# One decoder block on one core: how many expert rows go ahead of the second search, how densely they come in it, and on which engine

## The chip, the core and the metric

The kernel runs on one core of a Trainium2 chip, from a single launch. The time is the device time of that core in microseconds, from three runs. Beside them there is one execution under the hardware profiler. The engines are named as the profile names them: PE is TensorE, DVE is VectorE, ACT is ScalarE, POOL is GpSimd, SP is the engine that issues most transfers.

## What is computed

One decoder block on 512 tokens of width 1024: three token mixers side by side (forgetting attention, sliding-window attention, attention on a memory), merged by gates, and then product-key experts. The last part is what the change touches. For each token and each of 8 heads, 16 of 16384 experts are chosen by two searches over 128 half keys and a search over their sums; each expert is one row of `u` and one row of `v`.

```
s1 = einsum('bshd,hkd->bshk', q[..., 0, :], keys1);  v1, i1 = top_k(s1, 16)
s2 = einsum('bshd,hkd->bshk', q[..., 1, :], keys2);  v2, i2 = top_k(s2, 16)
cand = v1[..., :, None] + v2[..., None, :];          sv, si = top_k(cand, 16)
experts = i1[si // 16] * 128 + i2[si % 16];          gates = softmax(sv)
...
a = einsum('cd,ced->ce', h, u[experts])
out = einsum('ce,ced->cd', gelu(a) * gates, v[experts])
```

So each token has 128 experts. All is in float32.

## The kernel before

The tokens are four blocks of 128. Block 0 goes through the mixers by itself, then blocks 1 to 3 together. Its experts are therefore known early, and while the mixers of the other three run, block 0 is searched and its expert rows are worked off beside them.

**Two ways of doing the experts.** Blocks 0 and 1 gather rows: one indirect transfer of GpSimd's queue (L908) brings one row of `u` or `v` for each of 128 tokens, 512 KB. There are 512 such jobs, in the order block 0 `u` (0 to 127), block 0 `v` (128 to 255), block 1 `u` (256 to 383), block 1 `v` (384 to 511). Blocks 2 and 3 are dense: all 16384 rows of `u` (`dense_u`, L1078, 128 tiles) and of `v` (`dense_v`) are multiplied, and a gate matrix that is zero where an expert was not chosen picks the right ones.

**One row, the function `step`.** It first issues the gathers that may be ahead (four rows ahead of the one being worked off; five slots hold rows), then works off one row. For a row of `u` VectorE does a product with a sum (L929). For a row of `v` VectorE does a multiply-add: into `x1[0]`, which the order and the profile call `mg` and which lies in SBUF, as long as the mixers hold the PSUM banks (L936); after that into `two`, a PSUM tile (the first row writes it, L939, the others add, L942). A row called with `apart` is GpSimd's instead: for `v`, ScalarE scales the row (L932) and GpSimd adds it to `x1[0]` (L933). `two` is added to `x1[0]` after row 255 (L948).

**Stages, by the profile's times.**

- *End of the mixers, 562 to 622 us.* The generator `beside` works off rows up to `EARLY_ROWS`, whenever a weight load calls `pump`. With 184, rows 0 to 183 go here: 128 of `u`, 56 of `v`.
- *Second search, from 622 to about 741 us*, for blocks 1 to 3. For each head and half PE multiplies a weight tile of 512 KB, split into a high and a low part (ScalarE casts `whi`, L123; GpSimd subtracts `wlo`, L136), ScalarE copies the queries `qp` (L770), PE multiplies the keys (L774), ScalarE copies the scores `s` (L777). VectorE finds the best 16 of each (L731 to L735), GpSimd builds the 64 sums `cand` (L742), and VectorE finds the best 16 of those. Four tiles of `dense_u` lie in between.
- *Choosing, 741 to 825 us.* VectorE turns places into expert numbers (L828 to L872) for the three blocks, and 37 rows go among it; PE does `dense_u`.
- *Spreading, 825 to 985 us.* 64 times, VectorE builds one-hot matrices (`o`, L1144), ScalarE scales them (L1147), PE multiplies them (L1159), VectorE (L1162) and ScalarE (L1165) take the result; 60 rows and 23 tiles of `dense_u` go among it. There every fourth row is apart.
- *Final products, 985 us to the end.* 128 steps of `dense_v`, each with its share of what is left of `dense_u` and of the rows: the rows left are spread evenly over 124 steps.

**How often a row comes in the second search.** The search is a generator that names the cost of each piece of VectorE work in units: 1.6 for one block's best 16 of one half, 1.2 for one of the 64 sums. A head has 6 x 1.6 + 3 x 1.2 = 13.2 units, and the eight heads have 105.6. `spent` adds them up; `credit` does as well, and whenever it reaches `PER_ROW`, a row follows and `PER_ROW` is taken off. Each weight load calls `pump`, which finds nothing to do here and sets the credit to zero: that happens at the start of heads 0 to 5, whose turn loads the weights of the head after the next.

**What sets the order.** Up to the end of the search a scheduler places instructions by a simulated timeline; rows in the search have a low priority (`tc.high_priority(-LATER)`), so they fill gaps and may come later than where they were written. From there on POOL, DVE and PE run in the order in which the code is written.

Of the kernel before, what the change touches and what calls it, by code (L numbers as in the profile page):

```python
# [51 lines left out]
UNREAD = 36  # L52
LATER = 400
PACE = {"search": 20.0, "choose": 8.0, "rows": 3.5}
EARLY_ROWS, PER_ROW, APART, NO_APART = 184, 3.7, 4, 94.0
OWN_ROWS = 9


# [1 line left out]
def tile_block(ctx: ExitStack, tc: tile.TileContext, t: dict, out: bass.AP):  # L60
# [160 lines left out]
    def factors(sums, nb):  # L221

        ss = small_f(BIG, "rss", 2)[:, :nb]
        V.reduce_sum(ss, sums[:, :nb], axis=AX.X)
        return rsqrt_mean(ss, nb, D)

    def diagonals(r, nb):
        dg = small.tile([128, BIG, 128], F32, tag="dg", name="dg", bufs=1)
        for b in range(nb):
            A.activation(dg[:, b], ident, AF.Copy, scale=r[:, b:b + 1])  # L230
        return dg
# [646 lines left out]
    known, issued, done, ahead, flying, rpool = [2 * NJ], [0], [0], [AHEAD], {}, []  # L878
# [168 lines left out]
    def fetch_u_to(k):  # L1047
        while u_next[0] <= min(k, NK - 1):
            fetch_u(u_next[0])
            u_next[0] += 1  # L1050
# [36 lines left out]
    with tc.tile_pool(name="qb", bufs=2) as qq:  # L1087
        turn([x1[b] for b in GROUPS[1]], g2, *h2T)
        spent, dg, credit[0] = 0.0, None, 0.0
        for cost in search(qq, h2T, f, BIG):  # L1090
            spent += cost
            if dg is None and spent > 12.0:
                V.tensor_copy(rstd[:, 1:NB], factors(sums, BIG))
                dg = diagonals(rstd[:, 2:NB], ND)
                turn([x1[b] for b in DENSE], g2, h2f, None, dg)
            while u_next[0] < PRE_U and spent > 6.0 * u_next[0]:
                fetch_u_to(u_next[0])
            credit[0] += cost
            while credit[0] >= PER_ROW and NJ <= done[0] < known[0]:
                credit[0] -= PER_ROW  # L1100
                with tc.high_priority(-LATER):
                    step(apart=done[0] % APART == 0 and spent < NO_APART)
            if k_u < FIRST_U and spent > 104.0 / FIRST_U * (k_u + 1):
                list(dense_u(k_u))
                k_u += 1
# [317 lines left out]
```

## Time and profile before

| | |
|---|---|
| runs (us) | 1549.64, 1550.77, 1543.61; median 1549.64 |
| the profiled execution (us) | 1548.8 |
| its span, first to last instruction (us) | 1547.0 |
| mean granted clock of TensorE | 0.99 |
| data moved | 533.48 MB, mean 345 GB/s |
| rows of `v` on VectorE in PSUM (L942) | 197 |
| rows of `v` on GpSimd (L933) | 8 |

The profile gives, for each engine, its busy time in any stretch of the span; what ended each idle time of an engine (its waits); and a timeline of single instructions. A group of instructions is written as line, engine, operation, output and inputs, then how often it ran and how long. A busy TensorE is not TensorE at its peak, since its matmuls overlap and their ends are modelled.

### The profile page before, as it was taken

To read this page: it belongs to the slowest core of one execution; us is meant where nothing else is said; L and a number is where in the kernel's file an instruction comes from. 1 tells how busy PE (TensorE), PEld (TensorE's weight loads), DVE (VectorE), ACT (ScalarE), POOL (GpSimd) and SP (SyncE) were. 2 spreads that over 40 slices of the span, in tenths; PEclk is the share of its full clock that TensorE was granted. 3 is DMA by queue.
4 is the path that set the end of the run, shared out by engine and by line. 5 is a ranking of instruction groups with operands and counts; after the bars stand their busy time and mean duration, and the time that the engine had idled before them with its cause. 6 is when DMAs were issued, how large, how long until landed. Compare 5 with 4: busy or idle time off the path is not lost.

```text
span 1547.0 us, 27092 instructions
## 1 busy us (share of the span) xinstructions
PE 1498.3 (97%) x9411; PEld 1360.5 (88%) x9411; DVE 1419.4 (92%) x2673; ACT 812.4 (53%) x1806; POOL 778.1 (50%) x642
## 2 busy tenths in 40 slices
PE   8999999999999989999999999999999999999998
PEld 7999899997897989999888887788888888888887
DVE  6689488989999999999999999899999999999998
ACT  7778346646345533352225899545444544544543
POOL 1101016767667456877445666545554544555451
PEclk9999999999998999999999999999999999999999
DMA  8688657998999898986998999999999999999995
GB/s 325 207 289 300 246 174 280 338 362 302 360 367 325 293 356 317 352 310 232 327 365 329 393 395 384 373 397 398 401 410 403 408 410 404 411 410 410 410 410 209
DMA packets 180125, 533.48 MB, mean 345 GB/s; under 512 B 17660, under 2 KB 48148, under 8 KB 179988
## 3 DMA queue, kind: packets, MB, share of 16 engines
q0 software_dynamic: 73728, 268.47, 45.9%
q1 hardware_dynamic: 96180, 227.54, 40.1%
q10 hardware_dynamic: 10080, 35.75, 5.8%
q8 instruction: 74, 1.21, 0.3%
q14 instruction: 63, 0.52, 0.1%
HBM read 516.99 MB, written 14.69 MB: 344 GB/s over the span
## 4 chain that ended last, share of the span: by engine, by line
PE 52%; issue 14%; DMA 11%; POOL 9%; DVE 9%; ACT 4%; POOLq 0%; DVEq 0%; SPq 0%; ACTq 0%
PE mm L153 9%; PE mm L152 9%; PE mm L154 9%; POOL row L908 9%; PE mm L1078 5%; DMA row<-in_peer_v_dram,eidx 4%; DMA row<-in_peer_u_dram,eidx 3%; PE sc L1078 3%; DVE wlo L138 2%; DMA gd<-st 2%; PE mm L766 2%; DVE o L1144 2%; DVE scr L929 1%; PE tp L384 1%; PE sc L506 1%
## 5 line engine op out<-in xcount | busy, mean ns | idle before, releaser
L908 POOL DMA_INDIRECT row<-in_peer_v_dram,eidx x256 | 322.2, 1258 | 298.3 <-DVE two L942 175.5
L908 POOL DMA_INDIRECT row<-in_peer_u_dram,eidx x256 | 315.4, 1232 | 219.8 <-DVE scr L929 115.8
L138 DVE TENSOR_TENSOR wlo<-raw,whi 128x1024 fp32r<-128x1024 f32 (+1 forms) x228 | 277.2, 1220 | 21.7 <-ACT whi L123 17.5
L942 DVE SCALAR_TENSOR_TENSOR two<-row,acts,two 128x1024 f32<-128x1024 f32 x197 | 252.6, 1282 | 5.3 <-DMA row<-in_peer_v_dram,eidx 3.1
L123 ACT CAST whi<-raw 128x1024 fp32r<-128x1024 f32 x146 | 152.2, 1050 | 119.2 <-PE mm L153 75.4
L929 DVE SCALAR_TENSOR_TENSOR scr<-row,own 128x1024 bf16<-128x1024 f32 x128 | 156.2, 1220 | 7.1 <-DMA row<-in_peer_u_dram,eidx 6.4
L929 DVE SCALAR_TENSOR_TENSOR scr<-row,two 128x1024 bf16<-128x1024 f32 x115 | 139.5, 1213 | 3.8 <-DMA row<-in_peer_u_dram,eidx 2.9
L210 POOL TENSOR_TENSOR rsy<-rsv,mhalf 128x4 f32<-128x4 f32 (+5 forms) x25 | 37.8, 1515 | 177.2 <-DVE rsv L209 176.3
L1212 ACT CAST ah<-ga 128x256 fp32r<-128x256 f32 x116 | 47.1, 407 | 150.2 <-PE tp L153 125.0
L152 PE MATMUL mm<-hhi,whi 128*128 128x384 f32 x320 | 110.8, 346 | 1.8 <-ACT hhi L244 1.4
L153 PE MATMUL mm<-hlo,whi 128*128 128x384 f32 x320 | 110.7, 346 | 0.0
L154 PE MATMUL mm<-hhi,wlo 128*128 128x384 f32 x320 | 109.9, 343 | 0.0
L152 PE MATMUL mm<-whi,hhi 128*128 128x256 f32 (+1 forms) x360 | 103.6, 290 | 2.7 <-ACT hhi L681 1.9
L1214 ACT CAST whi<-raw 128x1024 fp32r<-128x1024 f32 x96 | 100.3, 1047 | 9.5 <-DMA raw<-in_peer_v_dram 4.6
L153 PE MATMUL mm<-wlo,hhi 128*128 128x256 f32 (+1 forms) x360 | 102.7, 286 | 1.3 <-DVE wlo L138 1.3
L153 PE MATMUL sc<-wlo,ah 128*128 128x512 f32 x256 | 101.2, 395 | 2.5 <-DVE wlo L138 2.5
L152 PE MATMUL sc<-whi,ah 128*128 128x512 f32 x256 | 100.8, 394 | 1.3 <-ACT whi L1214 1.2
L154 PE MATMUL mm<-whi,hlo 128*128 128x256 f32 (+1 forms) x360 | 102.0, 285 | 0.0
L154 PE MATMUL sc<-whi,al 128*128 128x512 f32 x256 | 101.2, 395 | 0.0
L153 PE MATMUL tp<-wlo,ah 128*128 128x512 f32 x256 | 101.1, 395 | 0.0
L152 PE MATMUL tp<-whi,ah 128*128 128x512 f32 x256 | 101.0, 395 | 0.0
L154 PE MATMUL tp<-whi,al 128*128 128x512 f32 x256 | 100.6, 393 | 0.0
(332 smaller groups left out, 4478.2 us busy)
## 6 DMA issues: line engine op xcount, KB each, us to landing
raw<-in_peer_v_dram SPq DMA_DIRECT2D x96, 512.0 KB
hhi<-in_uT_dram ACTq DMA_DIRECT2D x68, 512.0 KB
raw<-in_w_tr_dram SPq DMA_DIRECT2D x48, 512.0 KB
raw<-in_w_nat_dram SPq DMA_DIRECT2D x40, 512.0 KB
last<-in_peer_v_dram SPq DMA_DIRECT2D x32, 512.0 KB
hhi<-in_uT_dram SPq DMA_DIRECT2D x26, 512.0 KB
raw<-in_w_o_dram SPq DMA_DIRECT2D x24, 512.0 KB
gd<-st SPq DMA_DIRECT2D x24, 512.0 KB
```

The costliest lines, as they stand in the source:

```text
L123: ins = (cast or A.copy)(hi[:, :n * w], raw[:, :n * w])
L138: V.tensor_sub(lo, raw, hi.bitcast(F32))
L152: PE.matmul(ps, lh, rh, start=first, stop=False)
L153: PE.matmul(ps, lh, rl, start=False, stop=False)
L154: PE.matmul(ps, ll, rh, start=False, stop=last)
L210: G.tensor_tensor(y, v, mhalf[:, :n], op=OP.pow)
L908: ins = G.indirect_dma_start(out=r, out_offset=None, in_=t["peer_" + tab], in_offset=bass.IndirectOffsetOnAxis(ap=eidx[b][:, j:j + 1], axi ...
L929: V.scalar_tensor_tensor(scr, r, 1.0, two[0] if b else h2n[b], op0=OP.mult, op1=OP.mult, accum_out=acts[b][:, c]))
L942: V.scalar_tensor_tensor(two[0], r, acts[b][:, c], two[0], op0=OP.mult, op1=OP.add))
L1078: PE.matmul(ps[:, :TD], w[:, dc], h2f[dc], start=dc == 0, stop=dc == KC - 1)
L1212: A.copy(ah, a)
L1214: A.copy(hi, raw)
```

## The change

```diff
-EARLY_ROWS, PER_ROW, APART, NO_APART = 184, 3.7, 4, 94.0
+EARLY_ROWS, PER_ROW, NO_APART = 179, 3.2, 94.0
...
             while credit[0] >= PER_ROW and NJ <= done[0] < known[0]:
                 credit[0] -= PER_ROW
                 with tc.high_priority(-LATER):
-                    step(apart=done[0] % APART == 0 and spent < NO_APART)
+                    step(apart=done[0] % (4 if spent < 52.0 else 2) == 0 and spent < NO_APART)
```

Five rows fewer are worked off beside the mixers. In the search a row comes every 3.2 units instead of every 3.7. Up to 52 units every fourth row is GpSimd's, as before; from there to 94 units every second one is. The sum of rows is the same. The slots from which the last nine early rows may be served move with `EARLY_ROWS`: that is now so from row 170 on, not 175.

Since the scheduler decides, the order of the instructions says what moved. VectorE, at the end of the mixers' last transposes (L246) and the first search step of block 1 to 3, before the change:

```order
L246 SCALAR_TENSOR_TENSOR hlo<-sc,gcol,hhi 128x384
L942 SCALAR_TENSOR_TENSOR two<-row,acts_213,two 128x1024
L1093 COPY rstd<-rsy 128x3
L942 SCALAR_TENSOR_TENSOR two<-row,acts_213,two 128x1024 x2
L731 MAX v_7900<-s 128x8 x3
L942 SCALAR_TENSOR_TENSOR two<-row,acts_213,two 128x1024
L732 MAX_INDEX ids_7605<-v_7900,s 128x8
L733 MATCH_REPLACE tmp<-v_7900,s 128x128
L732 MAX_INDEX ids_7605<-v_7900,s 128x8 x2
L942 SCALAR_TENSOR_TENSOR two<-row,acts_213,two 128x1024
L734 MAX v_7900<-tmp 128x8
L735 MAX_INDEX ids_7605<-v_7900,tmp 128x8
```

and after it:

```order
L246 SCALAR_TENSOR_TENSOR hlo<-sc,gcol,hhi 128x384
L1093 COPY rstd<-rsy 128x3
L731 MAX v_7885<-s 128x8 x3
L732 MAX_INDEX ids_7590<-v_7885,s 128x8
L733 MATCH_REPLACE tmp<-v_7885,s 128x128
L732 MAX_INDEX ids_7590<-v_7885,s 128x8 x2
L734 MAX v_7885<-tmp 128x8
L735 MAX_INDEX ids_7590<-v_7885,tmp 128x8
L731 MAX v_7885<-s 128x8 x3
```

The five L942 rows that stood here are gone; one (four instructions further up) stays in both. VectorE at the search's end, where the choosing begins (L801, L828), before:

```order
L734 MAX best<-tmp 128x8
L735 MAX_INDEX pos<-best,tmp 128x8
L801 TENSOR_TENSOR ex<-best 128x384
L828 TENSOR_SCALAR sh<-pos 128x128
L829 TENSOR_SCALAR p_9180<-sh 128x128
L830 TENSOR_SCALAR sh<-pos 128x128
L831 CAST p_9181<-pos 128x128
L833 SCALAR_TENSOR_TENSOR p_9180<-sh,p_9180 128x128
L834 SCALAR_TENSOR_TENSOR ri<-p_9181,p_9180 128x128
L942 SCALAR_TENSOR_TENSOR two<-row,acts_213,two 128x1024
L836 TENSOR_SCALAR rj<-ri 128x128
```

and after:

```order
L735 MAX_INDEX pos<-best,tmp 128x8
L801 TENSOR_TENSOR ex<-best 128x384
L828 TENSOR_SCALAR sh<-pos 128x128
L829 TENSOR_SCALAR p_9191<-sh 128x128
L830 TENSOR_SCALAR sh<-pos 128x128
L831 CAST p_9192<-pos 128x128
L833 SCALAR_TENSOR_TENSOR p_9191<-sh,p_9191 128x128
L942 SCALAR_TENSOR_TENSOR two<-row,acts_213,two 128x1024
L834 SCALAR_TENSOR_TENSOR ri<-p_9192,p_9191 128x128
L942 SCALAR_TENSOR_TENSOR two<-row,acts_213,two 128x1024 x4
L836 TENSOR_SCALAR rj<-ri 128x128
```

Four more rows stand between the search and the choosing's main part. GpSimd in the last third of the search (`cand` are the sums, L908 the gathers, L933 the adds), before:

```order
L908 DMA row<-in_peer_v_dram,eidx_212 128x1024
L136 TENSOR_TENSOR wlo<-raw,whi 128x1024
L933 TENSOR_TENSOR mg_2281<-mg_2281,row 128x1024
L742 TENSOR_TENSOR cand<-v_8696 128x3x24
L742 TENSOR_TENSOR cand<-v_8696 128x3x16
L908 DMA row<-in_peer_v_dram,eidx_212 128x1024 x2
L742 TENSOR_TENSOR cand<-v_8696 128x3x8
L908 DMA row<-in_peer_v_dram,eidx_212 128x1024
L933 TENSOR_TENSOR mg_2281<-mg_2281,row 128x1024
L742 TENSOR_TENSOR cand<-v_8696 128x3x16
```

and after:

```order
L933 TENSOR_TENSOR mg_2281<-mg_2281,row 128x1024
L908 DMA row<-in_peer_v_dram,eidx_212 128x1024
L742 TENSOR_TENSOR cand<-v_8698 128x3x8
L742 TENSOR_TENSOR cand<-v_8698 128x3x16
L908 DMA row<-in_peer_v_dram,eidx_212 128x1024
L742 TENSOR_TENSOR cand<-v_8774 128x3x24
L742 TENSOR_TENSOR cand<-v_8774 128x3x16
L933 TENSOR_TENSOR mg_2281<-mg_2281,row 128x1024
L908 DMA row<-in_peer_v_dram,eidx_212 128x1024
L933 TENSOR_TENSOR mg_2281<-mg_2281,row 128x1024
L908 DMA row<-in_peer_v_dram,eidx_212 128x1024
```

Of ten rows two were adds; of eleven three are now, and a gather follows each.

## The prediction

> **What bounds the kernel now.** I read the page first, then the busy times by stage, then each engine's waits in the stages that the change touches.
>
> ```profile
> span 1547.0 us, 27092 instructions
> PE 1498.3 (97%) x9411; PEld 1360.5 (88%) x9411; DVE 1419.4 (92%) x2673; ACT 812.4 (53%) x1806; POOL 778.1 (50%) x642
> ```
>
> TensorE and VectorE are both nearly full, so an average says little; what counts is who is short in which stage. In the table by stage the columns are the stretch and its length, then the busy time of PE, PE's weight loads, DVE, ACT and POOL, then the granted clock, the DMA share and GB/s.
>
> ```profile
> core 0: us, PE busy (x) PEld busy (x) DVE busy (x) ACT busy (x) POOL busy (x), PEclk, DMA share, GB/s
> 562.00:622.00 60.00, 53.03 (x380) 50.57 (x378) 58.96 (x71) 23.92 (x49) 33.06 (x23) 0.96 0.90 321
> 622.00:637.00 15.00, 13.40 (x69) 12.98 (x70) 12.22 (x16) 5.46 (x10) 12.93 (x10) 0.83 0.93 321
> 637.00:741.00 104.00, 104.00 (x603) 99.97 (x602) 103.70 (x605) 37.42 (x63) 77.33 (x79) 1.00 0.80 293
> 741.00:825.00 84.00, 84.00 (x393) 73.93 (x392) 82.37 (x127) 16.24 (x44) 40.37 (x38) 1.00 0.97 361
> 825.00:985.00 160.00, 152.22 (x924) 133.89 (x922) 147.23 (x228) 138.18 (x507) 95.58 (x77) 0.99 1.01 368
> 985.00:1200.00 215.00, 212.71 (x1238) 186.80 (x1238) 205.27 (x288) 105.06 (x154) 107.71 (x80) 1.00 1.02 403
> 1200.00:1520.00 320.00, 316.99 (x1852) 278.94 (x1852) 318.06 (x323) 155.28 (x226) 161.61 (x118) 1.00 1.03 408
> ```
>
> The stages: the end of the mixers (562 to 622), a hinge (622 to 637), the second search (637 to 741), the choosing (741 to 825), the spreading of the gates (825 to 985), the final products (985 on). In the search and the choosing TensorE has no gap at all; VectorE has 0.3 and 1.6 us of gaps. In the hinge VectorE has 2.8 us of gaps. From 1200 on VectorE is short: 318.06 of 320.
>
> **The change, in rows.** Rows 128 to 255 are block 0's products with `v`. Counting the search's cost units, with the credit set to zero at each pair of weight loads, gives 25 rows in the search before (184 to 208, six of them GpSimd's) and 32 after (179 to 210, eleven GpSimd's). The 37 rows of the choosing follow, then 60 in the spreading: it now begins at row 248, not 246, and the final products at 308, not 306. GpSimd's adds go from 8 to 13 and VectorE's L942 rows from 197 to 192, which the two orders confirm.
>
> ```profile
> L942 DVE SCALAR_TENSOR_TENSOR two<-row,acts,two x197: 1260/1281/1291, 628.5 to 1528.4; 128x1024 f32<-128x1024 f32 x197
> L932 ACT ACTIVATE row<-row,acts x8: 1133/1146/1171, 660.1 to 844.6; 128x1024 f32<-128x1024 f32 x8
> L933 POOL TENSOR_TENSOR mg<-mg,row x8: 2343/2363/2404, 663.4 to 845.8; 128x1024 f32<-128x1024 f32 x8
> ```
>
> Over the whole kernel VectorE loses 5 rows of 1.28 us, 6.4 us. ScalarE gains 5 scalings of 1.15 us, 5.7 us, and GpSimd 5 adds of 2.36 us, 11.8 us. ScalarE's lie beside a search in which it is busy 37.42 of 104 us. The new order also splits one group of exponentials in the choosing, so that two activation tables are loaded once more.
>
> ```profile
> L1080 ACT ACT_TABLE_LOAD x1 | 1.3, 1283 | 0.0
> ```
>
> That is 2.6 us on an engine that is busy 16.24 of 84 us in the choosing, and I cost all of it at nothing; without that cover ScalarE's part would be 8.3 us.
>
> **Where VectorE's 6.4 us go.** Three rows less stand before the first choosing, none less in the choosing (37) and the spreading (45 on VectorE in both), two less in the final products. So there are two terms.
>
> *Term 1, the hinge and the search.* These are rows of VectorE's timeline, ScalarE's two first copies of scores, and TensorE's first spread; columns are start, duration, instruction and, in brackets, idle time before it.
>
> ```profile
> 632.02 0.16 DVE L1093 COPY rstd<-rsy 128x3 f32<-128x3 f32 x1
> 632.14 1.29 DVE L942 SCALAR_TENSOR_TENSOR two<-row,acts,two 128x1024 f32<-128x1024 f32 x1
> 636.21 1.29 DVE L942 SCALAR_TENSOR_TENSOR two<-row,acts,two 128x1024 f32<-128x1024 f32 x1 [2.78 <-DMA row<-in_peer_v_dram,eidx]
> 637.41 0.67 DVE L731 MAX8 v<-s 128x8 f32<-128x128 f32 x3
> 638.00 1.27 DVE L942 SCALAR_TENSOR_TENSOR two<-row,acts,two 128x1024 f32<-128x1024 f32 x1
> ...
> 640.24 1.27 DVE L942 SCALAR_TENSOR_TENSOR two<-row,acts,two 128x1024 f32<-128x1024 f32 x1
> ...
> 642.02 0.66 DVE L731 MAX8 v<-s 128x8 f32<-128x128 f32 x3
> ...
> 826.91 1.22 DVE L1144 TENSOR_TENSOR o<-tp,eT 128x1024 f32<-128x1024 f32 x1
> 828.05 0.28 DVE L1162 TENSOR_TENSOR ga<-sc,ga 128x128 f32<-128x128 f32 x1
> ```
> ```profile
> 635.62 0.47 ACT L777 COPY s<-sc 128x384 f32<-128x384 f32 x1
> 640.21 0.48 ACT L777 COPY s<-sc 128x384 f32<-128x384 f32 x1
> ```
> ```profile
> 824.93 1.05 PE L1159 MATMUL sc<-o 128*128 128x128 f32 x8
> ```
>
> An L942 holds VectorE for 1.20 us (636.21 to 637.41). Before the second tile of scores is searched (642.02) VectorE does six of them; after, by its order, one. But those five filled time in which VectorE had to wait for scores anyway. The first tile is there at 635.62 + 0.47 = 636.1, so the first MAX can start 1.3 us earlier. Between the two MAX groups lie 642.02 - 637.41 = 4.6 us, 2.4 of them two L942 rows; without them VectorE is ready for the second tile at 636.1 + 2.2 = 638.3 and waits 2.4 us for it, until 640.21 + 0.48 = 640.7. That is again 1.3 us ahead of before. From there to the choosing 25 - 6 = 19 L942 rows remain before and 22 - 1 = 21 after, two more: +2.4 us. VectorE has hardly a gap from there to 825, so it comes to its first L1144 at 826.9 **1.1 us later**, though it has fewer rows. Does anything wait for that? TensorE's first spread ends at 825.98 and VectorE takes it at 828.05, 2.1 us later: VectorE is the late one, and the 1.1 us are passed on into the spreading. The ends of this term: -2.1 us (VectorE earlier by all that TensorE leaves) and +1.1; I take +1.1 because it follows rows and order.
>
> *Term 2, the final products.* 206 rows were paced over 124 steps, 1.661 each; now 204, 1.645 each. While rows of `u` run (to about 1200) TensorE has 2.3 us of gaps in 215, and a row less is worth little. The 128 rows of `v` fill the last 77 steps, in which VectorE is full: 77 x 0.016 x 1.20 = 1.5 us. TensorE has room to follow:
>
> ```profile
> PE mm L154 <- DVE u L1067: 3.4, 6, 0.8
> PE sc L153 <- DVE wlo L138: 1.7, 2, 1.1
> PE mm L154 <- DVE ulo L1067: 1.3, 3, 0.5
> ```
>
> It waits 6.4 us for VectorE between 985 and the end. Ends: 0 (TensorE the bound after all) and -2.4 (both rows count in full); I take **-1.5**.
>
> *What I cost at nothing: GpSimd's part.* Its work in the search stage (637 to 741), by group:
>
> ```profile
> L136 POOL TENSOR_TENSOR wlo<-raw,whi 128x1024 fp32r<-128x1024 f32 x12 | 28.8, 2398 | 2.1 <-ACT whi L123 1.9
> L908 POOL DMA_INDIRECT row<-in_peer_v_dram,eidx x29 | 27.7, 954 | 22.8 <-DVE tmp L733 7.0 <-DVE pos L735 3.8 <-DVE best L731 2.4
> L933 POOL TENSOR_TENSOR mg<-mg,row 128x1024 f32<-128x1024 f32 x6 | 14.2, 2372 | 0.1
> L742 POOL TENSOR_TENSOR cand<-v 128x48 f32<-128x48 f32 (+2 forms) x32 | 8.2, 274 | 0.6 <-DVE v L734 0.2 <-issue 0.2
> ```
>
> These are 77 us of 104. Five adds bring 11.8 and at most seven more gathers 7 x 0.95 = 6.7: 96 of 104. It fits, just. Queued behind an add are `wlo` (TensorE's products wait for it), `cand` (VectorE's third pair of MAX waits for it) and the next gather. In the new order three `wlo` come first and gathers later, so that each `wlo` but the last stands behind less GpSimd work than before, and the last behind one add more, 2.4 us. Most of the gathers' idle time is waiting for VectorE to free a slot, so GpSimd has run ahead. The cost lies between 0 and 11.8; I take 0, with the second as a rival.
>
> *A rule against the change.* GpSimd arithmetic can hold VectorE up; VectorE's and GpSimd's timelines show both cases.
>
> ```profile
> 609.55 3.33 DVE L936 SCALAR_TENSOR_TENSOR mg<-row,acts,mg 128x1024 f32<-128x1024 f32 x1
> 619.36 2.54 DVE L936 SCALAR_TENSOR_TENSOR mg<-row,acts,mg 128x1024 f32<-128x1024 f32 x1
> 624.59 2.88 DVE L936 SCALAR_TENSOR_TENSOR mg<-row,acts,mg 128x1024 f32<-128x1024 f32 x1
> 727.85 1.27 DVE L942 SCALAR_TENSOR_TENSOR two<-row,acts,two 128x1024 f32<-128x1024 f32 x1
> ```
> ```profile
> 609.41 2.38 POOL L136 TENSOR_TENSOR wlo<-raw,whi 128x1024 fp32r<-128x1024 f32 x1 [3.82 <-ACT whi L123]
> 727.61 2.37 POOL L933 TENSOR_TENSOR mg<-mg,row 128x1024 f32<-128x1024 f32 x1
> ```
>
> L936 at 609.55, both of whose large operands are SBUF tiles, took 3.33 us beside a GpSimd subtraction; L942, whose accumulator `two` is a PSUM tile, took its usual 1.27 us beside an add. [...] It would cost where an add slides beside the choosing, whose operations read two SBUF tiles.
>
> **Sum.** 1548.8 us (the profiled execution) + 1.1 - 1.5 = **1548.4 us**. The runs shown have a median of 1549.64, 0.8 us above that execution, and lie between 1543.61 and 1550.77. About 0.5%, 7.7 us, is what a measurement of this kernel can tell from no change; the sum is far below it.
>
> **Rivals.**
>
> - *The whole saving is paid out*: 5 x 1.28 = 6.4 us, 1542.4. For it: VectorE has almost no gap from 637 to 985. Against: the hinge, where the moved rows stood, has the gaps. An order that also ends TensorE's 1.6 us of gaps there (13.40 of 15 us, at a granted clock of 0.83) would pass 0.5%.
> - *TensorE is the bound of the final products*: term 2 is 0, 1549.9. For it: no gap in most steps. Against: its 6.4 us of waits for VectorE.
> - *GpSimd becomes the bound of the search* (the slower side): its adds push `wlo` or `cand` back, and 11.8 us land on TensorE's gapless chain: 1560.2. It decides as soon as GpSimd's work in the stage passes 104 us; I count 96. Against it: no wait of TensorE for `wlo` in the search before.
> - *Adds beside two-SBUF operations*: the three stretched L936 took 2.92 us on average, 1.64 over their usual 1.28; five such would cost 8.2 us, 1556.6. For it: three of the new adds stand at the search's end. Against: GpSimd finishes them before the choosing if it is on time.
>
> **Chances.** Forecast 0.51, whole saving 0.17, TensorE bound 0.12, GpSimd bound 0.13, adds beside the choosing 0.07. The range reaches from just below the whole saving to the fourth rival, 1541.5 to 1556.5, and leaves out half of the whole-saving case's spread (0.08) and most of the GpSimd case (0.10). Over 0.5% faster is only that first part with a little of the forecast's spread: 0.09. Over 0.5% slower is GpSimd's case and half of the last: 0.14. Within: 0.77.
>
> **What would show it.** In the changed profile: 13 L933 and 192 L942; a first MAX of the search near 636 and a gap of VectorE of about 2 us before the second tile's MAX; no TensorE wait for `wlo` and none of VectorE for `cand`; POOL near 95 of 104 us; the first L1144 about 1 us later than 826.9 and TensorE's chain still without a gap up to there; from 1200 on VectorE still full. A first L1144 before 826 refutes term 1; a gap of TensorE between 637 and 825 means that GpSimd, or the order, has cost more than I gave it.

## The result, and the profile after

The changed kernel takes 1563.77 us, the median of 8 runs (1560.21 to 1571.59); the kernel before took 1550.2 in the 8 runs beside them (1543.61 to 1559.02). The ratio is 1.0089, with a 95% interval of 1.007 to 1.0108. It is slower by about 13.5 us where 1548.4 was forecast; the range ended at 1556.5.

The page's span and engine totals of the changed kernel:

```profile
span 1560.8 us, 27101 instructions
PE 1501.2 (96%) x9411; PEld 1364.8 (87%) x9411; DVE 1419.9 (91%) x2668; ACT 819.6 (53%) x1813; POOL 795.5 (51%) x647
```

Its busy times by stage, with the columns and cuts of the prediction's table:

```profile
622.00:637.00 15.00, 12.75 (x62) 11.16 (x61) 11.90 (x14) 5.13 (x11) 12.34 (x9) 0.78 0.93 332
637.00:741.00 104.00, 104.00 (x606) 100.26 (x605) 96.20 (x592) 42.24 (x69) 83.68 (x80) 1.00 0.80 280
741.00:825.00 84.00, 79.94 (x364) 69.81 (x364) 81.02 (x122) 20.44 (x46) 44.66 (x39) 0.98 0.94 348
...
1200.00:1520.00 320.00, 318.01 (x1862) 280.11 (x1861) 318.36 (x324) 155.11 (x227) 164.68 (x119) 1.00 1.02 407
```

VectorE has 5 rows less and is as busy as before in total (1419.9 and 1419.4 us), and in the search it now has 7.8 us of gaps (96.20 of 104) where it had 0.3. GpSimd is busy 83.68 us of that stage, not the 96 that the prediction counted at most, and two of its adds run behind it: it isn't full.

Where the time goes is read from VectorE's timeline, of which these are the rows that matter (start, duration, instruction, idle time before it and what ended that):

```profile
621.21 3.52 DVE L936 SCALAR_TENSOR_TENSOR mg<-row,acts,mg 128x1024 f32<-128x1024 f32 x1
...
633.13 0.60 DVE L246 SCALAR_TENSOR_TENSOR hlo<-sc,gcol,hhi 128x384 fp32r<-128x384 f32 x1
634.76 0.17 DVE L1093 COPY rstd<-rsy 128x3 f32<-128x3 f32 x1 [1.03 <-POOL rsy L210]
638.51 0.68 DVE L731 MAX8 v<-s 128x8 f32<-128x128 f32 x3 [3.58 <-ACT s L777]
...
643.12 0.68 DVE L731 MAX8 v<-s 128x8 f32<-128x128 f32 x3 [2.29 <-ACT s L777]
...
726.43 1.29 DVE L942 SCALAR_TENSOR_TENSOR two<-row,acts,two 128x1024 f32<-128x1024 f32 x1 [3.92 <-DMA row<-in_peer_v_dram,eidx]
...
742.05 2.72 DVE L801 TENSOR_TENSOR ex<-best 128x384 f32<-128x384 f32 x1
...
747.06 2.32 DVE L834 SCALAR_TENSOR_TENSOR ri<-p,p 128x128 f32<-128x128 f32 x1
...
751.86 4.03 DVE L942 SCALAR_TENSOR_TENSOR two<-row,acts,two 128x1024 f32<-128x1024 f32 x3 [1.28 <-DMA row<-in_peer_v_dram,eidx]
...
840.26 1.22 DVE L1144 TENSOR_TENSOR o<-tp,eT 128x1024 f32<-128x1024 f32 x1
841.39 0.28 DVE L1162 TENSOR_TENSOR ga<-sc,ga 128x128 f32<-128x128 f32 x1
```

and of the kernel before the row that the account below begins with, and the two that are compared there:

```profile
630.31 0.60 DVE L246 SCALAR_TENSOR_TENSOR hlo<-sc,gcol,hhi 128x384 fp32r<-128x384 f32 x1
...
739.53 0.56 DVE L801 TENSOR_TENSOR ex<-best 128x384 f32<-128x384 f32 x1
...
741.12 0.29 DVE L834 SCALAR_TENSOR_TENSOR ri<-p,p 128x128 f32<-128x128 f32 x1
```

**The account** is kept on VectorE, which takes the first spread 2.1 us after TensorE has it ready in the kernel before. From the start of the last L246 to the start of the first L1162 its stretch took 828.05 - 630.31 = 197.7 us before and takes 841.39 - 633.13 = 208.3 now, 10.6 us more. It is the sum of four things: L942 rows at 1.2 us each, waits in the hinge (the first 14 us), waits behind it, and all other work. What follows the stretch is counted up to the start of VectorE's last work (L1331).

| | rows | hinge waits | later waits | other work | total | behind it, to VectorE's last L1331 |
|---|---|---|---|---|---|---|
| before | 61 = 73.2 | 2.8 | 0.0 | 121.8 | 197.7 | 714.6 |
| changed | 58 = 69.6 | 6.9 | 5.2 | 126.6 | 208.3 | 715.1 |

(The sums agree within 0.1.) Three rows less bring 3.6 us, and the hinge takes 4.1 more of waits: 1.03 + 3.58 + 2.29 = 6.9, where it had 2.8. That is the trade which the prediction made. What it didn't have are the waits for rows in transit, 3.92 + 1.28 = 5.2 us, and 4.8 us more of "other work", nearly all in two instructions: L801 took 0.56 us before and takes 2.72, L834 took 0.29 and takes 2.32. Such a stretch counts as busy, so no view of waits shows it; it is found by comparing durations of the same instruction.

Of the rest, 2.8 us stand at the last L246 already. 2.0 of them are there at 313 us, where the two programs have done the same, and 0.8 come at the L936 at 621.21, which took 3.52 us, not 2.54. In the profiled executions of seven other kernels that are the kernel before up to there, the last L246 begins anywhere from 628.5 to 635.0 us, so nothing here shows that the change makes these 2.8 us.

GpSimd's rows of the timeline show what lay beside L801 and L834:

```profile
717.80 0.95 POOL L908 DMA_INDIRECT row<-in_peer_v_dram,eidx  x1 [1.79 <-DVE ids L735]
...
737.06 2.36 POOL L933 TENSOR_TENSOR mg<-mg,row 128x1024 f32<-128x1024 f32 x1
...
741.97 2.37 POOL L933 TENSOR_TENSOR mg<-mg,row 128x1024 f32<-128x1024 f32 x1
...
746.87 2.35 POOL L933 TENSOR_TENSOR mg<-mg,row 128x1024 f32<-128x1024 f32 x1
```

The adds of the last two apart rows run from 741.97 and 746.87, in the choosing. L801 ends at 744.77 and L834 at 749.38, 0.4 and 0.2 us after those adds.

For the wait at 726.43 the issues of transfers tell more (tile, queue, count, KB each, median us from issue to landing), in three stretches: 637 to 715, 716 to 718.5, 716 to 724.

```profile
row<-in_peer_v_dram,eidx POOLq DMA_INDIRECT x19, 5.6
...
row<-in_peer_v_dram,eidx POOLq DMA_INDIRECT x1, 8.6
...
hhi<-in_uT_dram SPq DMA_DIRECT2D x2, 512.0 KB, 8.4
hlo<-in_uT_dram SPq DMA_DIRECT2D x2, 512.0 KB, 12.3
row<-in_peer_v_dram,eidx POOLq DMA_INDIRECT x3, 8.4
```

The gather issued at 717.80 landed 8.6 us later, at 726.4, and there the L942 began. From 715 on six tiles of `u` (three `hhi`, three `hlo`) are fetched at once, and a gather beside them takes 8.4 us, not 5.6.

### The profile page after: what moved, and what is told of

Its sections match the earlier page's. It is cut to its first block, busy times and chain, and to the rows that moved or that the text cites. A ratio compares the mean times of both kernels' runs of the same rounds, so it can differ in the third digit from the quotient of the medians.

```text
span 1560.8 us, 27101 instructions
## 1 busy us (share of the span) xinstructions
PE 1501.2 (96%) x9411; PEld 1364.8 (87%) x9411; DVE 1419.9 (91%) x2668; ACT 819.6 (53%) x1813; POOL 795.5 (51%) x647
## 4 chain that ended last, share of the span: by engine, by line
PE 19%; issue 11%; DVE 9%; POOL 8%; DMA 4%; ACT 1%; POOLq 0%; DVEq 0%; ACTq 0%
POOL row L908 8%; PE mm L1078 4%; DVE two L942 3%; PE sc L1159 3%; DMA row<-in_peer_u_dram,eidx 2%; PE mm L154 2%; DMA row<-in_peer_v_dram,eidx 2%; PE mm L153 1%; PE mm L152 1%; PE sc L153 1%; PE sc L154 1%; PE tp L153 1%; PE tp L152 1%; PE sc L152 1%; PE tp L154 1%
## 5 line engine op out<-in xcount | busy, mean ns | idle before, releaser
L908 POOL DMA_INDIRECT row<-in_peer_v_dram,eidx x256 | 327.7, 1280 | 285.0 <-DVE two L942 186.4
L908 POOL DMA_INDIRECT row<-in_peer_u_dram,eidx x256 | 314.0, 1227 | 226.0 <-DVE scr L929 126.7
L942 DVE SCALAR_TENSOR_TENSOR two<-row,acts,two 128x1024 f32<-128x1024 f32 x192 | 246.4, 1283 | 7.5 <-DMA row<-in_peer_v_dram,eidx 5.2
```

Of the source, the lines that this page charges most:

```text
L908: ins = G.indirect_dma_start(out=r, out_offset=None, in_=t["peer_" + tab], in_offset=bass.IndirectOffsetOnAxis(ap=eidx[b][:, j:j + 1], axi ...
L942: V.scalar_tensor_tensor(two[0], r, acts[b][:, c], two[0], op0=OP.mult, op1=OP.add))
```

## The experiments

Each is an edit of the changed kernel or of the kernel before, as said, and is compared with runs of the kernel before on the same chip. First the accounts of all, each from one profiled execution. "Sum" is total plus behind, less the 912.3 us of the kernel before. The account and the runs agree within 7 us, most within 3; the profiled executions of e6 and o2 lie 7 and 5 us under the medians of their runs. What stands behind the stretch varies from 713.3 to 722.5 us among the nine kernels that have as many rows left there as the changed one (changed, e8d, s1, o1, o2, b1, o3, c1, c2), so a few us in that column are not explained by rows.

Letters in the expectations name theories. A, B and the first D are said below; S, R and G say why rows come late: GpSimd's rows keep their slots too long (S), five slots are too few where rows follow each other closely (R), or GpSimd's time delays the gathers (G). D in the last three runs is another one, the transfers of `u`.

| kernel | rows | hinge | later | other | total | behind | sum | median us | ratio [95%] |
|---|---|---|---|---|---|---|---|---|---|
| e6_only_rows | 56 | 6.9 | 0.7 | 122.1 | 196.9 | 721.6 | +6.2 | 1563.6 | 1.0071 [1.0049, 1.0093] |
| e5_only_pace | 67 | 2.7 | 3.2 | 122.1 | 208.5 | 715.4 | +11.6 | 1562.5 | 1.0076 [1.0053, 1.01] |
| e7_only_adds | 59 | 4.6 | 8.2 | 122.2 | 205.8 | 713.0 | +6.5 | 1555.9 | 1.0022 [1.0004, 1.0039] |
| e1_every_fourth | 62 | 6.9 | 3.5 | 122.1 | 206.9 | 715.9 | +10.5 | 1560.6 | 1.0067 [1.0045, 1.009] |
| e3_rows_back | 64 | 3.1 | 2.8 | 122.6 | 205.3 | 717.0 | +10.0 | 1561.7 | 1.0077 [1.0051, 1.0103] |
| e8d_adds_early | 58 | 6.9 | 12.1 | 123.7 | 212.2 | 714.6 | +14.5 | 1570.8 | 1.0118 [1.0094, 1.0142] |
| m3_beside | 61 | 2.9 | 0.0 | 128.1 | 204.2 | 715.6 | +7.5 | 1557.3 | 1.0041 [1.0021, 1.006] |
| m4_load | 61 | 4.3 | 1.1 | 122.2 | 200.8 | 716.2 | +4.7 | 1554.4 | 1.0017 [1.0001, 1.0032] |
| s1_slot_freed | 58 | 7.0 | 3.9 | 124.8 | 205.3 | 722.5 | +15.5 | 1566.8 | 1.0111 [1.0094, 1.0129] |
| s2_freed_184 | 58 | 3.5 | 2.6 | 122.4 | 198.2 | 716.2 | +2.1 | 1551.2 | 1.0001 [0.9989, 1.0014] |
| o1_last_left_out | 58 | 6.9 | 7.9 | 122.3 | 206.7 | 719.7 | +14.1 | 1562.4 | 1.0067 [1.0045, 1.0088] |
| o2_first_left_out | 58 | 7.0 | 4.4 | 122.8 | 203.7 | 713.3 | +4.7 | 1556.9 | 1.0038 [1.0023, 1.0054] |
| b1_unbunched | 58 | 6.9 | 4.2 | 126.3 | 207.0 | 715.7 | +10.4 | 1560.4 | 1.0056 [1.0034, 1.0078] |
| o3_both | 58 | 6.9 | 5.4 | 122.5 | 204.4 | 714.3 | +6.4 | 1559.3 | 1.0048 [1.003, 1.0066] |
| r4_before | 59 | 5.2 | 2.7 | 122.1 | 200.7 | 740.0 | +28.4 | 1584.1 | 1.0229 [1.0194, 1.0263] |
| c1_after_one_by_one | 58 | 6.9 | 9.3 | 124.0 | 209.8 | 716.0 | +13.5 | 1562.0 | 1.0066 [1.0042, 1.009] |
| c2_b1_one_by_one | 58 | 6.9 | 2.5 | 126.1 | 205.1 | 721.2 | +14.0 | 1563.1 | 1.007 [1.0044, 1.0096] |
| c3_e7_one_by_one | 59 | 3.2 | 2.6 | 123.7 | 200.3 | 715.3 | +3.3 | 1555.2 | 1.0022 [1.0001, 1.0044] |

### Each part by itself

The first theory was that the three adds at the search's end cost it all (A); its rivals were the moved rows (B) and the number of adds (D).

```diff
-EARLY_ROWS, PER_ROW, APART, NO_APART = 184, 3.7, 4, 94.0
+EARLY_ROWS, PER_ROW, NO_APART = 179, 3.7, 94.0   e6
+EARLY_ROWS, PER_ROW, NO_APART = 184, 3.2, 94.0   e5
+EARLY_ROWS, PER_ROW, NO_APART = 184, 3.7, 94.0   e7
...
-                    step(apart=done[0] % APART == 0 and spent < NO_APART)
+                    step(apart=done[0] % 4 == 0 and spent < NO_APART)   e5, e6
+                    step(apart=done[0] % (4 if spent < 52.0 else 2) == 0 and spent < NO_APART)   e7
```

> The kernel before, with 179 rows ahead of the search and nothing else changed: a row every 3.7 units, every fourth apart (6 adds). Theory A: the first MAX of the search starts about 1.3 us earlier against the last transposes, VectorE waits about 2 us for the second score tile, the first L1144 comes 1.3 us earlier; five rows more in the final products cost up to 3.7 us: 1549 to 1553.5. Rival B (moving the five rows out of the hinge is the cost): 1557 or more.

> The kernel before, with every second row apart from 52 to 94 units and nothing else changed: 8 adds, not 6, two of which come after the last sums. Theory A: two rows less on VectorE, -2.4 us, but the last two adds stretch one or two operations of the choosing (about 2.1 us each) and may make VectorE wait for a row: 1550 to 1557, with L801 or L834 over 1.5 us. Rival B: 1550.2 - 2.4 = 1547.8, nothing stretched.

> The kernel before, with a row every 3.2 units and nothing else changed: 7 rows more in the search, 1 of them apart. By the account: 67 rows of 1.2 before the first L1162, 2.8 us of hinge waits, 0 to 3.5 us of waits for rows: 205 to 209 us there, not 197.7; behind it seven rows less. If VectorE sets the end of the final products the 7 us come back (5 rows of VectorE's, 6.4 us): 1551 to 1555; if TensorE does, they don't: 1558 to 1562.

Each part alone makes the kernel slower, and each in another way; for e7 the interval nearly reaches no change. Five rows later (e6): the stretch up to the first L1162 is 0.8 us shorter, near the 1.3 that the prediction reckoned for the hinge, but behind it 7.0 us are added. A had bounded that at 3.7 and gave 1549 to 1553.5: a miss. B's range (1557 or more) held, so by the kernels' times the five rows alone cost nearly as much as the whole change; why they cost it behind the first L1162 is not shown. Rows closer together (e5): six rows of VectorE's more and a wait of 3.2 make 10.8 us ahead, and the seven rows fewer behind bring nothing (715.4 and 714.6), the case of the expectation in which TensorE sets the end of the final products. More adds (e7): two rows less on VectorE, but 8.2 us of waits; nothing is stretched. VectorE's waits in e7, behind the hinge (engine, tile and line, what it waited for, us in total, times, longest):

```profile
DVE two L942 <- DMA row<-in_peer_v_dram,eidx: 7.1, 4, 3.2
DVE best L731 <- POOL cand L742: 1.1, 1, 1.1
```

Two at a time, the changed kernel without the dense adds (e1: every fourth row apart throughout) and with the five rows back ahead of the search (e3: `EARLY_ROWS` 184):

> The changed kernel, but every fourth row apart throughout the search: 7 adds of GpSimd in it, not 11, none of them after the search. Theory A (three adds that stand at the search's end cost 9.4 us: 5.2 us of VectorE's waits for late rows, 4.2 us of two stretched operations): these go, and VectorE has four rows more, 4 x 1.2 us: 1563.8 - 9.4 + 4.8 = about 1559; L801 takes 0.56 us and L834 0.29 us again; no wait for a row over 1 us. Rival B (the five rows moved out of the hinge, and two rows more before the choosing, are the cost; adds help VectorE): 1563.8 + 4.8 = about 1569.

> The changed kernel with 184 rows ahead of the search again (32 rows in it, 10 of them apart). By the account of VectorE: 64 rows of 1.2 before the first L1162 (58 in the changed kernel), hinge waits of 2.8 us again and not 6.9, waits for rows of 5 to 8 us and stretches of 0 to 4.6 us since the dense adds stay: 207 to 214 us from the last L246 to the first L1162; behind it seven rows less. Theory: 6 us less there if VectorE sets the end of the final products, so 1553 to 1561; 1560 to 1567 if TensorE does. Rival B (the five rows moved out of the hinge are the cost): close to before, 1549 to 1553.

Neither is close to the kernel before. In e1 nothing is stretched and the waits shrink to 3.5 us, 1.9 of them for rows and 1.6 for a constant table, but VectorE does four rows more; in e3 the hinge is as before, and the six rows and 2.8 us of waits remain. The parts don't add up (0.71 + 0.76 + 0.22% against 0.89%). The first sends five rows behind the first L1162 and the second takes seven ahead of it, which may be why; no run shows it.

### The adds: their place, their number, and what they do to VectorE

The eleven adds early, two rows of three up to 56 units:

```diff
+                    step(apart=done[0] % 3 > 0 and spent < 56.0)
```

> The changed kernel, with its 11 adds of GpSimd in the search placed early: two rows of three are apart up to 56 units, none behind that. Same rows, same pace, same count. Theory A (the place of the adds, the three at the search's end, costs 9.4 us): 1563.8 - 9.4 = about 1554; first L1144 near 798. Rival D (the count costs: 11 adds are more than GpSimd has room for, wherever they stand): no change, 1562 to 1566, and waits of VectorE for rows or of TensorE for wlo in the first half of the search in place of those at its end. Rival B (the moved rows): no change, 1562 to 1566, without such waits.

It is the slowest of the kernels up to here, so the place alone isn't it. VectorE's waits behind the hinge:

```profile
DVE two L942 <- DMA row<-in_peer_v_dram,eidx: 7.0, 8, 2.7
DVE v L731 <- ACT s L777: 5.0, 3, 2.6
```

Then adds with no rows behind them, in the kernel before: five in the choosing (m3), three in the search's second half (m4).

```diff
                 step()
+                if done[0] % 6 == 0 and done[0] < 240:                       m3
+                    G.tensor_tensor(x1[0], x1[0], x1[0], op=OP.add)
...
                     step(apart=done[0] % APART == 0 and spent < NO_APART)
+                    if done[0] % 4 == 3 and spent > 52.0:                    m4
+                        G.tensor_tensor(x1[0], x1[0], x1[0], op=OP.add)
```

> The kernel before, with five more adds of GpSimd (x1[0] to itself, so block 0's output is not the reference's) spread over the choosing, one behind every sixth row; nothing else changed. Theory (an add stretches the operations of the choosing that read two SBUF tiles until it ends, as L801 and L834 in the changed kernel): each add costs VectorE 1 to 2.2 us, its work other than rows goes from 122 to 127 to 133 us, single operations of 0.3 to 1.2 us take 2 us and more, and the first L1162 comes 5 to 11 us later; the kernel 1555 to 1561. Rival (no contention; those two operations were slow for a reason of their own): other work stays at 122 us, at most a wait for a row, the kernel within 2 us of before.

> The kernel before, with three more adds of GpSimd (x1[0] to itself, 128x1024, so block 0's output is not the reference's) behind rows 198, 202 and 206, where the change has adds; VectorE's rows stay as they are, and no row's slot is held by these adds. From the last L246 to the first L1162 VectorE took 197.7 us before: 61 rows of 1.2, 2.8 of waits, 122 of other work. Theory G (an add that stands in GpSimd's queue delays the gathers behind it, and VectorE waits for their rows): 3 to 8 us more of waits for rows, 201 to 206, and 1553 to 1559 for the kernel. Rival S (not GpSimd's time but the slots, which a row of GpSimd's keeps through scaling and adding): waits under 2 us, 198 to 200, no change of the kernel's time.

m3 shows the stretch by itself: 6.3 us more of other work, no wait at all, and the kernel 0.41% slower. VectorE's and GpSimd's timelines of m3 (L1250 is the added line):

```profile
747.23 2.02 DVE L846 CAST rb<-ri 128x128 bf16<-128x128 f32 x1
759.54 2.03 DVE L846 CAST rb<-rj 128x128 bf16<-128x128 f32 x1
...
747.20 1.91 POOL L1250 TENSOR_TENSOR mg<-mg 128x1024 f32<-128x1024 f32 x1
759.54 1.90 POOL L1250 TENSOR_TENSOR mg<-mg 128x1024 f32<-128x1024 f32 x1
```

A cast of 0.26 us that begins with an add ends with it. m4 shows the other half: no wait for a row, 1.1 us of others, so the time of three adds on GpSimd does not by itself make rows late. (That spoke for S; the slots are tried below.) Its add at 739.50 lay beside the search's last steps, and none of them is longer than elsewhere:

```profile
739.45 0.21 DVE L733 MATCH_REPLACE8 tmp<-best,cand 128x64 f32<-128x64 f32 x1
739.64 0.22 DVE L732 FIND_INDEX8 pos<-best,cand 128x8 uint32<-128x64 f32 x1
739.78 0.33 DVE L734 MAX8 best<-tmp 128x8 f32<-128x64 f32 x2
...
740.23 1.27 DVE L942 SCALAR_TENSOR_TENSOR two<-row,acts,two 128x1024 f32<-128x1024 f32 x1
...
739.50 1.91 POOL L1104 TENSOR_TENSOR mg<-mg 128x1024 f32<-128x1024 f32 x1
```

### Adds left out

The changed kernel without GpSimd's adds of the last three apart rows (o1), or of the eight ahead of them (o2):

```diff
-            G.tensor_tensor(x1[b], x1[b], r, op=OP.add)
+            if not 202 <= n <= 206:      o1 (o2: not 180 <= n <= 200)
+                G.tensor_tensor(x1[b], x1[b], r, op=OP.add)
```

> The changed kernel without GpSimd's adds of rows 202, 204 and 206, the last three of the search (ScalarE still scales these rows; they are left out of block 0's sum). VectorE's 58 rows and all else stay. Theory (what the change lost it lost to these three adds: 4.6 us of stretched operations of the choosing and most of 5.2 us of waits for rows): from the last L246 to the first L1162 VectorE takes 198 to 203 us, not 208.3, its other work is back at 122 us, and the kernel takes 1553 to 1559. Rival (they only happen to stand there; the loss is in the moved rows or in all eleven adds): 206 to 209 us, 1560 to 1565.

> The other half: the changed kernel without GpSimd's adds of rows 180 to 200 (eight; they are left out of block 0's sum), while those of rows 202, 204 and 206 stay. Theory (the last three adds alone make the loss): the stretch stays, 2 to 4.6 us, and the waits for rows are 2 to 5 us: 203 to 208 us, 1558 to 1564. Rival (the count of adds makes the waits): no wait for a row over 1 us; what is left is at most the stretch: 199 to 203 us, 1553 to 1558.

The stretch goes in o1 (122.3), but the total falls only from 208.3 to 206.7, since the waits for rows rise to 7.9: what VectorE no longer loses in the choosing it then waits for rows. Here theory A falls. VectorE's timeline of o1 where the choosing begins (a line further down than in the changed kernel):

```profile
743.33 1.28 DVE L943 SCALAR_TENSOR_TENSOR two<-row,acts,two 128x1024 f32<-128x1024 f32 x1
746.48 1.29 DVE L943 SCALAR_TENSOR_TENSOR two<-row,acts,two 128x1024 f32<-128x1024 f32 x1 [1.87 <-DMA row<-in_peer_v_dram,eidx]
750.03 1.29 DVE L943 SCALAR_TENSOR_TENSOR two<-row,acts,two 128x1024 f32<-128x1024 f32 x1 [2.26 <-DMA row<-in_peer_v_dram,eidx]
```

Here stands the stack that the order showed (`L942 x4` between L834 and L836): rows that had slid out of the search, with nothing between them. In o2 the waits are 4.4 us, 3.3 of them for rows, and no operation is as long as L801 was (the longest takes 1.34 us, L801 again); it lies between the two expectations.

### Slots

Slots freed as soon as ScalarE has scaled the row, in the second search alone, with the changed kernel's adds (s1) and with 184 rows and nine adds (s2); and one slot less in the kernel before (r4).

```diff
-            tc.keep_in_program_order(A.activation(r, r, AF.Copy, scale=acts[b][:, c]))
-            G.tensor_tensor(x1[b], x1[b], r, op=OP.add)
+            scr = big.tile([128, D], BF16, tag="junk", name="scr")           s1, s2
+            tc.keep_in_program_order(A.activation(scr, r, AF.Copy, scale=acts[b][:, c]))
+            G.tensor_tensor(x1[b], x1[b], scr, op=OP.add)
...
-AHEAD, ROWS_IN, MORE = 4, 5, 2
+AHEAD, ROWS_IN, MORE = 3, 4, 2                                               r4
```

> The changed kernel, but in the second search ScalarE writes the scaled row of an apart step into a scratch tile (bfloat16, so these rows are rounded) and GpSimd adds from there: a row's slot is free after ScalarE's 1.15 us, not after GpSimd's add. Number and place of the adds are as in the change. Theory S (waits for rows come from slots that rows of GpSimd's hold): waits after the hinge fall from 5.2 us to under 1.5 us, and from the last L246 to the first L1162 VectorE takes 199 to 205 us, not 208.3; 1555 to 1560. Rival G (GpSimd's time delays the gathers): 207 to 209 us, 1562 to 1565.

> The kernel before (184 rows, one every 3.7 units), with the scratch tile of the run beside it, and every second row apart from 21 to 75 units, every fourth elsewhere: 9 adds, not 6, and none after the search's last sums. Theory S: 58 rows of VectorE's before the first L1162, hinge waits 2.8 us, waits for rows under 1.5 us, nothing stretched: 194 to 196 us, not 197.7; 1548 to 1551. Rival G: waits of 4 to 8 us, 198 to 203 us, 1552 to 1557.

> The kernel before with four slots for rows and three rows ahead, not five and four; the number and the kinds of the rows are the same, the order shifts a little (59 rows of VectorE's between the last L246 and the first L1162, not 61). Theory R: waits of VectorE for rows appear in the search and the choosing, 3 to 10 us after the hinge, where there were none: 198 to 206 us to the first L1162 with two rows less (2.4 us). Rival G: the slots don't matter, waits under 1 us, 195 to 196 us.

The waits in s1 fall from 5.2 to 3.9, not under 1.5, and the kernel is no faster. Both that are left (1.6 and 2.3 us) stand where the choosing begins, and none near 92 us behind the last L246, where the changed kernel waits. This doesn't refute S: the rows whose gather the semaphores tell apart wait 14 to 34 us from the gather's issue until ScalarE scales them (six rows of s1), and they keep their slots for that time here too. In r4 VectorE waits for no row behind the hinge (its 2.7 us are for scores and for a constant table of the choosing, and there are 3.0 us for a row in the hinge), so one slot less doesn't by itself make rows late there. What r4 loses it loses behind the first L1162 (740.0 and 714.6). s2 was the try for a kernel better than both: the same time as before, with 1.8 us of waits for rows and 198.2 us where Theory S gave under 1.5 and 194 to 196.

### Unstacked rows, and six transfers one by one

b1 lets the choosing take the four stacked rows, with the same counts; o3 also leaves out the last three adds.

```diff
-            while credit[0] >= PER_ROW and NJ <= done[0] < known[0]:
+            while credit[0] >= PER_ROW and NJ <= done[0] < 207:
-AMONG, UNWEIGHED = 1.0, 14
+AMONG, UNWEIGHED = 0.9, 14
```

> The changed kernel, but the search calls no row behind row 206, and the choosing takes its rows at 0.9 units each, not 1.0, so that it takes the four rows more: the same 58 rows of VectorE's and the same adds, only the four rows that stood in one stack where the choosing begins are spread over it. Theory R (a stack of rows is faster than five slots can bring them): no wait for a row where the choosing begins (1.3 us in the changed kernel, 4.1 us with the last adds left out), the wait near 93 us after the last L246 stays: 205 to 207 us to the first L1162, not 208.3; 1560 to 1563. Rival G (GpSimd's adds delay the gathers): waits as before, 4 to 6 us, 208 us, 1563 to 1565.

> The run beside it, and GpSimd's adds of rows 202, 204 and 206 left out too (these rows are missing in block 0's sum). Theory R: neither stretched operations (other work 122 us) nor a stack: waits for rows of 0 to 4 us, 198.5 to 202.5 us to the first L1162; 1554 to 1558. So the two causes, each of which alone brings little, bring 6 to 10 us together. Rival (the rows are late for a reason behind both): waits of 5 to 8 us, 204 to 207 us, 1560 to 1563.

b1 came out as R had it: the wait where the choosing begins is gone, the one near 92 us stays (4.2), 207.0 us. o3 reaches 204.4, less than the 198.5 to 202.5 expected: 4.2 us of that wait and 1.3 for the constant table are left. So the wait near 92 us has a cause of its own, and it stands where the six tiles of `u` are fetched. The last three runs fetch those one by one, from ScalarE's queue, each with a tile of `dense_u`: in the changed kernel (c1), in b1 (c2) and in e7 (c3).

```diff
-            fetch_u_to(min(max(k, PRE_U) + URING - 1, LAG) if k < LAG else k)
+            fetch_u_to((PRE_U + min(k - FIRST_U, URING - 1) if k < PRE_U else min(k + URING - 1, LAG)) if k < LAG else k)
-        if k > LAG + 2:
+        if k > LAG + 2 or k < PRE_U + URING:
             tc.keep_in_program_order(nc.scalar.dma_start(u_raw[k], t["uT"][k]))
```

> The changed kernel, but the six tiles of u that fill hhi and hlo at the search's end are fetched one by one, one with each dense_u tile (from ScalarE's queue), not all at once. The scheduler moves some of VectorE's rows by it; their number (58) stays. Theory D (gathers beside the six transfers land after 8 us and more, so VectorE waits): the wait of 3.9 us near 92 us after the last L246 goes (under 1 us); the stack of rows and the stretched operations stay: 203 to 206 us to the first L1162, not 208.3; 1558 to 1561. Rival (rows late for another reason): the wait stays, 207 to 209 us, 1562 to 1565.

> The same one-by-one fetch in the kernel whose choosing takes the four stacked rows (207.0 us to the first L1162, one wait of 4.2 us for a row). Theory D: no wait for a row over 1 us after the hinge: 202 to 204 us; 1555 to 1558. Rival: the wait of 4 us stays, 206 to 208 us, 1560 to 1562.

> The same one-by-one fetch in the kernel before with only the denser adds (184 rows, 3.7 units; 205.8 us to the first L1162, 8.2 us of waits after the hinge, 59 rows of VectorE's). Theory D: waits after the hinge of 1 to 4 us: 197 to 201 us; 1548 to 1552, so no slower than before. Rival: 7 us or more of waits, 204 to 206 us, 1553 to 1557.

VectorE's waits for rows behind the hinge in c1:

```profile
DVE two L942 <- DMA row<-in_peer_v_dram,eidx: 9.3, 6, 4.7
```

in c2:

```profile
DVE two L942 <- DMA row<-in_peer_v_dram,eidx: 2.5, 2, 1.4
```

and in c3:

```profile
DVE two L942 <- DMA row<-in_peer_v_dram,eidx: 2.3, 3, 1.3
```

In c1 the wait near 92 us is 0.2 us, as D had it, but the scheduler now stacks five rows where the choosing begins, and there 9.0 us of waits arise, nearly all of the 9.3. They don't measure the stack alone: the six transfers now stand there (96.7 to 115.1 us behind the last L246), and the gathers issued among them from 103.7 to 114.8 us took 7.8 to 10.0 us. With both remedies (c2) 2.5 of 5.2 us are left, in two waits of 1.4 and 1.1 where D gave none over 1; in c3 the waits behind the hinge fall from 8.2 to 2.6. The kernels' times do not follow by as much: c2 loses 6 us behind the first L1162 (721.2 and 715.1), which no run here explains, and c3's ratio is e7's. c1, c2 and c3 are all slower than D's ranges. No run joins all three remedies (the last adds left out, the rows unstacked, the transfers one by one); with two of them each, o3 takes 1559.3 us and c2 1563.1.

**How far ahead a row is gathered.** The kernel before fetches the same six tiles at the same place and doesn't wait. Its trace names no landing of a gather, but every trace holds the packets of the transfers and the semaphore that a row of VectorE's waits for, and from these the gathers can be followed (in the changed kernel a gather's last packet comes 0.3 to 0.7 us ahead of the landing that its trace gives here). The three issued 82 to 90 us behind the last L246 took 6.1, 7.4 and 7.0 us from issue to last packet in the kernel before, and 8.3, 7.4 and 8.0 in the changed kernel: slow in both. What differs is how long before its use a row is gathered. For VectorE's rows from 80 to 110 us, the time from the gather's issue until VectorE was ready for the row was:

| kernel | rows | median, us | least, us |
|---|---|---|---|
| before | 7 | 10.7 | 8.8 |
| e6_only_rows | 7 | 12.3 | 9.4 |
| m4_load | 7 | 12.3 | 8.0 |
| e7_only_adds | 4 | 6.5 | 4.1 |
| changed | 4 | 6.0 | 4.7 |

So before, the lead of a gather covered the slow transfers, and with the dense adds (e7 and the changed kernel) it doesn't. In e5 the least lead is 5.6 us, and there the gathers issued beside the six transfers are four and took 8.4 to 11.2 us. GpSimd's time alone doesn't shorten the lead, since m4, whose adds hold no row, has 12.3 us; whether the slots do or the order of the gathers among GpSimd's work, no run separates. Each line is one execution of a few rows.

## Why the prediction was wrong

- *GpSimd's part at nothing* ("The cost lies between 0 and 11.8; I take 0") is the step that failed, and with it "VectorE has hardly a gap from there to 825", from which the 1.1 us followed. The first L1144 came 13.3 us later (840.26 and 826.91), 2.8 of which stand at the last L246 already. The term was bounded at 0 to 11.8 us by GpSimd's load; VectorE paid 5.2 us of waits for rows and 4.8 us of longer operations, 10.0 us. The argument asked only whether GpSimd has the time, and it has (83.68 of 104). It did not ask what VectorE waits for besides: the rows in transit. Nor are these waits the adds' alone, since the dense pace without dense adds (e5) has 3.2 us of them.
- *Stretched operations*: the fourth rival, with a chance of 0.07, had this mechanism right, though only two of its five adds came to it and it priced no wait. It was set aside with "GpSimd finishes them before the choosing if it is on time"; two adds ran in the choosing and cost 2.16 + 2.03 us. m3 shows the price apart from the change, 6.3 us for five adds.
- *Waits for rows* were in no rival. Two causes are shown: the stack where the choosing begins (1.3 us, gone in b1; 4.1 us in o1, gone in o3) and the six `u` tiles' transfers (3.9 us, 0.2 in c1, where their gathers took 4.0 to 5.2 us and not 7.4 to 8.3). The stack stood in the order that the prediction quotes; it said that four rows more stand there, and not that rows in a stack must also arrive in one.
- *The hinge* was right: first MAX 5.4 us after the last L246, not 7.1 (1.3 earlier was forecast, it is 1.7), and a gap of 2.29 us before the second tile's MAX (2.4 forecast).
- *The final products*, -1.5: 212.5 + 356.0 us before, from the end of the spreading on, and 208.6 + 359.4 now (up to and from the first L939), -0.5. With fewer rows left the even spacing lets the 128 rows of `v` begin earlier and take longer. The term was mis-sized by 1.0 us and lies near its upper end, 0; in the column of the accounts a few us there are unexplained anyway.
- *ScalarE's part at nothing*: its cover did break. ScalarE stood idle for 8.26 us until a late row was there for L932, and the exponentials and the evacuation of `dense_u` came only after it; TensorE waited 4.1 us for that evacuation. A gap of TensorE between 637 and 825 was one of the prediction's own signs of being wrong. ScalarE's timeline and TensorE's waits between 741 and 825:

```profile
742.51 1.15 ACT L932 ACTIVATE row<-row,acts 128x1024 f32<-128x1024 f32 x1 [8.26 <-DMA row<-in_peer_v_dram,eidx]
...
747.84 0.38 ACT L1080 ACTIVATE ga<-sc 128x256 f32<-128x256 f32 x1
```
```profile
PE sc L1078 <- ACT ga L1080: 4.1, 1, 4.1
```

  It has no term in the account, because VectorE comes later still; had VectorE been on time, it might have been the next bound, which no run here shows.
- *The sum's best case.* Without waits for rows and without a stretch the changed kernel's account would be 69.6 + 6.9 + 122 = 198.5 us, 0.8 more than before, and 715.1 behind: about 1 us slower. So even undisturbed the change had nothing to win, which the prediction saw (-0.4), and 10 us to lose, which it priced at nothing.

What stays open: by which way the adds shorten the lead of the gathers in e7 and in the changed kernel, why five rows moved by themselves (e6) cost 12.7 us by the medians, and what makes the times behind the first L1162 differ by up to 9 us among kernels with as many rows there. More than five slots were not tried.

## What to carry to other kernels

When work goes from a full engine to a half-idle one, ask not only whether that engine has the time, but where its new work will stand when it runs late, which instructions of other engines it lengthens there, and whether the inputs of what the full engine keeps still arrive in time. Rows of low priority that a scheduler lets slide end up in a stack, and a stack needs its transfers landed in advance. A transfer that is slow is no harm while it is issued early enough: look at the time from issue to use, and not only at the time from issue to landing. Keep an account of the bounding engine (counted work, waits, everything else) between two fixed instructions: it shows stretched instructions, which no list of waits does, and it gave here within 7 us what each kernel took.

## What the runs showed of the hardware

- An operation needs no second SBUF input to be held up by GpSimd: the cast L846 (one input, 0.26 us) took 2.02 us beside an add (m3), while in m4 MAX8, FIND_INDEX8, MATCH_REPLACE8 and L942 beside an add were as fast as elsewhere (0.33 us for two, 0.22, 0.21 and 1.27). The Trainium skill, page "SBUF — State Buffer", section "Who interferes with whom", says that copies, casts and scalar-operand operations can run in a mode that uses both port pairs, and that whoever issues first keeps the shared pair for its whole instruction. m3 agrees: the cast begins with the add and ends 0.1 us after it.
- GpSimd's 128x1024 add took 2.37 us with two different float32 tiles (changed kernel), 1.90 with the same tile as both inputs (m3).
- A row's gather landed 5.6 us after issue in the search of the changed kernel (median of the 17 of 19 whose landing is recorded) and 8.4 us beside six transfers of 512 KB (three gathers). With those transfers moved away (c1) the gathers there took 4.0 to 5.2 us to their last packet.
